# The place of operands and the order of six products in a trunk of split matmuls

## The chip, the cores and the metric

One core of a Trainium2 chip runs the whole program in one launch. The metric is the device time of one execution in microseconds; the median of three runs is compared.

## What is computed

One step of a decoder trunk of one layer, for 256 prompt tokens and 32 sample tokens (288 columns in all), width 2048:

```python
x = x + 0.5 * rmsnorm(swiglu(rmsnorm(x, g[0]), ffn1_w_in, ffn1_w_out), g[1])
m, sg, sh = hybrid_mixer(rmsnorm(x, g[2]), mix_w_in, ..., mix_w_out, s_gla, s_hgrn)
x = x + rmsnorm(m, g[3])
x = x + 0.5 * rmsnorm(swiglu(rmsnorm(x, g[4]), ffn2_w_in, ffn2_w_out), g[5])

def swiglu(x, w_in, w_out):
    gate, up = jnp.split(x @ w_in, 2, axis=-1)
    return (jax.nn.silu(gate) * up) @ w_out
```

All inputs are float32; the hidden width of the SwiGLU is 5632, and the mixer projects 2048 to 7184, runs two gated linear recurrences and projects back. Nearly all of the work is in these projections.

## The kernel before

**Tiling.** Activations stand transposed: a tile has 128 features on the partitions and the 288 tokens as columns. A weight unit is 1024 columns wide on 128 partitions: two k tiles of 512 output features each (or, in some stages, two times 256). It is loaded by SyncE into `raw`, and split into a high part, written by ScalarE as a rounded copy, and a low part, the rest, written by VectorE; both go into a `wh` buffer (four of them, and two more at stage borders). Activations are split in the same way, into `xh` and `xl` for the sixteen x tiles, and `hh` and `hl` for the four hidden tiles of a chunk of 512 hidden features.

**Products.** A block makes four output tiles (f = 0 to 3) of 128 features in four PSUM buffers. For each unit, each f and each k of the unit's two, `mm` records the three products of `mm3`: high weight by high x (L621), high weight by low x (L622), low weight by high x (L623). Each is one matmul of 288 columns with its own weight load. In some units (those named in `byk`, where tiles of x have only just been made, or evictions are still under way) k is the outer loop and f the inner one. The first units of two blocks at the borders between sub-layers are recorded by `Fill`, for x tiles that are early there. The FFN runs over eleven chunks: gate, up, and the output products of the chunk before.

**Places.** `columns` cuts the 288 columns into `PLACES` = 4 pieces of 72, and `turns_of` makes a matmul read four neighbouring columns (a `LINE` of four elements) of each piece in turn. `pairs` interleaves two k tiles, so that the pieces of one tile stand 144 elements apart. The results land in PSUM by the same pattern, 72 elements apart, and so in the natural order. The low tiles start one line behind the high ones, and unused elements (tiles named `gap`, and spare columns) set where the weights begin: in lines of four elements and modulo 16, a weight stands 6 lines behind the high x and 5 behind the low x that it meets.

**Order.** Each engine runs its list in the order in which the code recorded it; `tick` and `issue_after` interleave the other engines' work with a block's units.

Of the kernel before, what the change touches and what calls it, by code (L numbers as in the profile page):

```python
# [9 lines left out]
F32 = mybir.dt.float32  # L10
F32R = mybir.dt.float32r
# [5 lines left out]
P = 128  # L17
TP = 256
TS = 32
T = TP + TS  # L20
# [3 lines left out]
KT = D // P  # L24
# [6 lines left out]

RAW_BUFS = 3
HL_BUFS = 4
HALF = 1024 + 8
LINE = 4
PLACES = 4


def columns(t):

    return t.rearrange("p (g c) -> p g c", g=PLACES)


def turns_of(t):

    return t.rearrange("p g (i e) -> p i g e", e=LINE)


def pairs(pool, n, names):

    parts = []
    for at, name in zip((0, LINE), names):
        t = pool.tile([P, n * T + 16 * at], F32R, name=name, tag=name.split("_")[0])[:, at:at + n * T]
        t = t.rearrange("p (k g j c) -> p k g j c", g=PLACES, j=2, c=T // PLACES)
        parts.append([t[:, k // 2, :, k % 2, :] for k in range(n)])
    return parts

SCAN_LAG = 4
X_EARLY = 12


class Weights:


    def __init__(self, tc, rawp, hlp):
        self.tc, self.nc, self.rawp, self.hlp = tc, tc.nc, rawp, hlp
        self.srcs, self.raws, self.parts = [], {}, {}
        self.loaded = self.split = self.used = 0
        self.last = {}
        self.extra, self.extra_units = None, ()  # L70
        self.behind = None
# [2 lines left out]

        self.extra, self.extra_units = pool, units

    def add(self, src):
        self.srcs.append(src)

    def load(self):  # L80
        i, src = self.loaded, self.srcs[self.loaded]
# [27 lines left out]
    def pieces(self, n):  # L109

        i = self.split
        raw = self.raws.pop(i)
        pool = self.extra if i in self.extra_units else self.hlp
        hl = pool.tile([P, 2112], F32R, name=f"wh{i}", tag="wh")[:, 0:2 * HALF].rearrange("p (a c) -> p a c", a=2)
        h, l = hl[:, :, 0:512], hl[:, :, 512:1024]
        self.parts[i] = (h, l)
        self.split += 1
        raw = raw.rearrange("p (a b) -> p a b", b=512)
        for j in range(n):
            a = slice(0, 2) if n == 1 else slice(2 * j // n, 2 * j // n + 1)  # L120
            w = min(512, 1024 // n)
            c = slice(j * w % 512, j * w % 512 + w)
            i1 = self.nc.scalar.activation(h[:, a, c], raw[:, a, c], AF.Copy).ins  # L123
            i2 = self.nc.vector.tensor_tensor(l[:, a, c], raw[:, a, c], h[:, a, c].bitcast(F32), op=ALU.subtract).ins  # L124
            self.recent = i1, i2
            yield i1, i2
# [27 lines left out]
def trunk_kernel(ctx, tc, x_prompt, x_sample, state_gla, state_hgrn, norm_gains, f1_in, f1_out, f2_in, f2_out,  # L154
# [6 lines left out]
    xpool = ctx.enter_context(tc.tile_pool(name="xpool", bufs=1))  # L161
    rawp = ctx.enter_context(tc.tile_pool(name="rawp", bufs=RAW_BUFS))
    hlp = ctx.enter_context(tc.tile_pool(name="hlp", bufs=HL_BUFS))
    hlp.tile([P, 40], F32, name="gap_w", bufs=1)
    mmp = ctx.enter_context(tc.tile_pool(name="mmp", bufs=5, space=PSUM))
    aux = ctx.enter_context(tc.tile_pool(name="aux", bufs=3, space=PSUM))
    sqp = ctx.enter_context(tc.tile_pool(name="sqp", bufs=2))
# [34 lines left out]
    def block_units(w, col, k0, nk, width=512):  # L202
        per = 1024 // width
        for k in range(k0, k0 + nk, per):
            W.add(w[k * P:(k + per) * P, col:col + width].rearrange("(k p) c -> p k c", p=P))

    def pair_units(w, col0, col1, nk):

        for k in range(0, nk, 2):
            W.add([(256 * i, w[k * P:(k + 2) * P, c:c + 256].rearrange("(k p) c -> p k c", p=P))  # L210
                   for i, c in enumerate((col0, col1))])

    def ffn_ops():

# [56 lines left out]
    EARLY = 4  # L271
    x = [xpool.tile([P, T], F32, name=f"x{k}") for k in range(KT)]
    yg = [xpool.tile([P, 4, T], F32, name=f"y{k}") for k in range(4)]
    y = [yg[k // 4][:, k % 4, :] for k in range(KT)]
    xh, xl = pairs(xpool, KT, ("xh", "xl"))
    rt = xpool.tile([P, T], F32, name="rt")
    rp = xpool.tile([P, T], F32, name="rp")
    acc = xpool.tile([P, T], F32, name="acc")
# [256 lines left out]
    class Fill:  # L535
# [3 lines left out]
        def __init__(self, pool, name, gains, gnext, some, ahead):  # L539
            self.gnext, self.name, self.some, self.ahead = gnext, name, some, ahead  # L540
            pool.tile([P, 8], F32, name=f"{name}gap")

            self.tiles = [list(zip(*pairs(pool, EARLY, (f"{name}{n}h", f"{name}{n}l")))) for n in "xy"]
            self.gains = pool.tile([P, 24], F32, name=f"{name}g")[:, 0:EARLY]
            V.tensor_tensor(self.gains, gains[:, 0:EARLY], prm[:, gnext * KT:gnext * KT + EARLY], op=ALU.mult)

        def old(self):
# [63 lines left out]
    def block(name, nk, rhs, evac, width=512, tick=None, tail=1, hold=False, most=99, fill=None, late=0, byk=(), lag=0, skip=()):  # L611

        nf, per = width // P, 1024 // width
        nu = nk // per
        ps = [mmtile(f"{name}_{f}") for f in range(nf)]
        ws = [W.next() for _ in range(EARLY // per)] if fill else []

        def mm3(dst, w, f, k, parts, start, stop):
            a, c = k % per, slice(f * P, f * P + P)
            dst, parts = turns_of(columns(dst)), [turns_of(t) for t in parts]  # L620
            yield lambda: PE.matmul(dst, w[0][:, a, c], parts[0], start=start, stop=False)  # L621
            yield lambda: PE.matmul(dst, w[0][:, a, c], parts[1], start=False, stop=False)  # L622
            yield lambda: PE.matmul(dst, w[1][:, a, c], parts[0], start=False, stop=stop)  # L623

        def mm(w, f, k):
            if not fill or f or k >= EARLY:
                for ready in mm3(ps[f][:, 0:T], w, f, k, rhs(k), k == 0, k == nk - 1):
                    product[0] = ready().ins

        if fill:  # L630
            fill.products(lambda dst, k, parts, stop: mm3(dst, ws[k // per], 0, k, parts, k == 0, stop), ps[0][:, 0:T])
        for u in range(nu - tail):
            w = ws.pop(0) if ws else W.next()
            if u not in byk:
                for f in range(nf):
                    for k in range(u * per, (u + 1) * per):
                        mm(w, f, k)
                    if tick is not None and f % 2:
                        tick(u * per + f // 2)
            for k in range(u * per, (u + 1) * per) if u in byk else ():  # L640
                if fill and k < UPDATED:

                    fs = range(1 if k < EARLY else 0, nf)
                    threes = [list(mm3(ps[f][:, 0:T], w, f, k, rhs(k), k == 0, False)) for f in fs]
                    for three in threes:
                        three[0]()
                        product[0] = three[2]().ins
                    with tc.issue_after(product[0]):
                        for three in threes:
                            product[0] = three[1]().ins  # L650
                elif k < late:

                    threes = [list(mm3(ps[f][:, 0:T], w, f, k, rhs(k), k == 0, False)) for f in range(nf)]
                    for ready in [r for t in threes for r in t[:2]] + [t[2] for t in threes]:
                        product[0] = ready().ins
                else:
                    for f in range(nf):
                        mm(w, f, k)
                if tick is not None:
                    tick(k)  # L660
            if u not in skip and not (lag and u == nu - tail - 1):
                W.ahead(most)
            if fill and u == 5:
                fill.scaled()
        ws = [W.next() for _ in range(tail)]
        ks = range((nu - tail) * per, nk)
        ticked = 0
        for f in range(nf):
            for k in ks:
                mm(ws[k // per - (nu - tail)], f, k)  # L670
            ins = evac(f, fill.total(ps[f][:, 0:T]) if fill and f == 0 else ps[f][:, 0:T])
            while tick is not None and (ticked + 1) * nf <= (f + 1) * len(ks):
                tick(ks[ticked])
                ticked += 1
            if lag and f == lag:
                with tc.issue_after(ins):
                    W.ahead(most)
        if not hold:
            W.ahead()
# [4 lines left out]
    def ffn(tag, gcol, gnext, pn, before, fill=None):  # L684
# [2 lines left out]
        border = []  # L687
        with ExitStack() as pools:
            fp = pools.enter_context(tc.tile_pool(name=f"ffn{tag}", bufs=2))
            fp.tile([P, 24], F32, name=f"gap_f{tag}", bufs=1)  # L690
            hid, final_tiles = {}, []

            def do_in(c):
                hh, hl = pairs(fp, 4, (f"hh{tag}_{c}", f"hl{tag}_{c}"))
                hid[c] = (hh, hl)
                gs = []

# [1003 lines left out]
    class Border:  # L1701


        def __init__(self, n, gains, gnext, some, ahead=0):
            self.pools = ExitStack()
            top = self.pools.enter_context(tc.tile_pool(name=f"top{gnext}", bufs=1, side="right"))
            top.tile([P, 80], F32, name=f"gap{gnext}")
            W.begin_extra(self.pools.enter_context(tc.tile_pool(name=f"hx{gnext}", bufs=2, side="right")), wider(n))
            self.fill = Fill(self.pools.enter_context(tc.tile_pool(name=f"fl{gnext}", bufs=1, side="right")),
                             f"fill{gnext}", gains, gnext, some, ahead)  # L1710
# [47 lines left out]
```

## Time and profile before

| | |
|---|---|
| median of 3 runs | 2159.18 us (2158.32 to 2159.96) |
| the profiled execution | 2157.96 us |
| its span, first to last instruction | 2156.2 us |
| TensorE busy | 2144.9 us (99%) |
| VectorE busy | 1382.0 us (64%) |
| ScalarE busy | 1017.1 us (47%) |
| HBM over the span | 174 GB/s |
| mean granted TensorE clock | 1.000 |

Matmuls are pipelined: a row of the profile gives some 0.29 us for one, while the next begins about 0.13 us after it. The distance between starts is the figure to read. A name such as `wh<-raw` is the tile written and the tile read; L with a number is a line of the kernel, which for products is the line in `mm3`.

### The profile page before, as it was taken

Reading aid. Unit: us, or ns where it says so; the run is one execution under the profiler, and the core shown is the slowest. Engines: PE = TensorE matmul, PEld = TensorE weight load, DVE = VectorE, ACT = ScalarE, POOL = GpSimd, SP = SyncE. Lnnn points to the kernel's source line nnn. Section 1 sums busy time; section 2 is a strip of 40 time slices with the busy share of each in tenths; the row PEclk is TensorE's granted clock in tenths of the full one; section 3 lists DMA queues with packets and bytes.
Section 4 is the critical chain, followed back from the end, with each engine's and each line's share of the span. In section 5 each row is a group of like instructions: output and inputs, shape, how many; then the busy total and the mean of one; then the engine's idle time right before and its main releaser. Section 6 shows DMA issues by size and latency. Waiting matters only on the chain.

```text
span 2156.2 us, 43224 instructions
## 1 busy us (share of the span) xinstructions
PE 2144.9 (99%) x17828; PEld 2126.5 (99%) x17828; DVE 1382.0 (64%) x2253; ACT 1017.1 (47%) x1537; POOL 180.6 (8%) x327
## 2 busy tenths in 40 slices
PE   9999999999999999999999999999999999999998
PEld 9999999999999999999999999999999999999998
DVE  7656546555565568888888755854655466556656
ACT  6453433343344345655676654544434333433344
POOL 2000000000000001333210000000000020122005
PEclk9999999999999999999999999999999999999999
DMA  7655555555556554678666564556555665666556
GB/s 224 181 172 175 174 173 173 176 172 174 173 176 186 177 175 142 195 211 221 177 191 181 181 194 139 167 176 174 170 175 175 171 184 177 184 183 185 176 168 164
DMA packets 227334, 384.87 MB, mean 178 GB/s; under 512 B 21362, under 2 KB 60864, under 8 KB 227136
## 3 DMA queue, kind: packets, MB, share of 16 engines
q1 hardware_dynamic: 213872, 365.02, 57.0%
q0 software_dynamic: 10992, 16.77, 2.9%
q8 instruction: 140, 2.29, 0.4%
q10 hardware_dynamic: 2272, 0.31, 0.1%
q14 instruction: 58, 0.48, 0.1%
HBM read 363.75 MB, written 11.80 MB: 174 GB/s over the span
## 4 chain that ended last, share of the span: by engine, by line
PE 94%; DVE 3%; ACT 2%; DMA 1%; issue 1%; DVEq 0%; ACTq 0%; SPq 0%
PE gate L621 10%; PE gate L622 9%; PE gate L623 9%; PE out L621 8%; PE out L622 8%; PE out L623 8%; PE up L621 8%; PE up L622 8%; PE up L623 8%; PE hfq L621 2%; PE mo L621 1%; PE hfq L622 1%; PE hfq L623 1%; PE mo L623 1%; PE mo L622 1%; ACT wh L123 1%
## 5 line engine op out<-in xcount | busy, mean ns | idle before, releaser
L124 DVE TENSOR_TENSOR wh<-raw,wh 128x1024 fp32r<-128x1024 f32 (+1 forms) x676 | 822.1, 1217 | 579.9 <-ACT wh L123 577.7
L123 ACT ACTIVATE wh<-raw 128x1024 fp32r<-128x1024 f32 (+1 forms) x676 | 710.1, 1052 | 899.0 <-PE gate L623 282.5
L621 PE MATMUL gate<-xh,wh 128*128 128x288 f32 x1660 | 479.8, 290 | 0.6 <-ACT wh L123 0.4
L623 PE MATMUL gate<-xh,wh 128*128 128x288 f32 x1660 | 476.4, 288 | 0.0
L622 PE MATMUL gate<-xl,wh 128*128 128x288 f32 x1660 | 475.6, 289 | 0.1
L621 PE MATMUL up<-xh,wh 128*128 128x288 f32 x1408 | 406.8, 289 | 0.0
L621 PE MATMUL out<-hh,wh 128*128 128x288 f32 x1408 | 406.7, 289 | 0.0
L622 PE MATMUL up<-xl,wh 128*128 128x288 f32 x1408 | 405.9, 288 | 0.0
L622 PE MATMUL out<-hl,wh 128*128 128x288 f32 x1408 | 405.9, 288 | 0.0
L623 PE MATMUL up<-xh,wh 128*128 128x288 f32 x1408 | 405.8, 288 | 0.0
L623 PE MATMUL out<-hh,wh 128*128 128x288 f32 x1408 | 405.7, 288 | 0.0
L621 PEld LDWEIGHTS gate<-xh,wh 128*128 128x128 f32 x1660 | 311.0, 188 | 1.7 <-ACT wh L123 0.6
L622 PEld LDWEIGHTS gate<-xl,wh 128*128 128x128 f32 x1660 | 310.2, 188 | 1.1 <-DVE xl L287 0.8
L623 PEld LDWEIGHTS gate<-xh,wh 128*128 128x128 f32 x1660 | 311.0, 188 | 0.2 <-DVE wh L124 0.2
L623 PEld LDWEIGHTS up<-xh,wh 128*128 128x128 f32 x1408 | 264.3, 188 | 0.0
L623 PEld LDWEIGHTS out<-hh,wh 128*128 128x128 f32 x1408 | 264.3, 188 | 0.0
L621 PEld LDWEIGHTS out<-hh,wh 128*128 128x128 f32 x1408 | 264.2, 188 | 0.0
L621 PEld LDWEIGHTS up<-xh,wh 128*128 128x128 f32 x1408 | 264.2, 188 | 0.0
L622 PEld LDWEIGHTS up<-xl,wh 128*128 128x128 f32 x1408 | 264.1, 188 | 0.0
L622 PEld LDWEIGHTS out<-hl,wh 128*128 128x128 f32 x1408 | 264.0, 188 | 0.0
L807 DVE TENSOR_TENSOR y<-out,y 128x288 f32<-128x288 f32 x287 | 118.4, 452 | 75.7 <-PE out L623 75.6
L764 POOL DMA_DIRECT2D xT<-b x64 | 37.2, 588 | 739.1 <-PE gate L623 553.7
(417 smaller groups left out, 2542.5 us busy)
## 6 DMA issues: line engine op xcount, KB each, us to landing
raw<-in_ffn_w_in_dram SPq DMA_DIRECT2D x350, 512.0 KB, 3.7
raw<-in_ffn_w_out_dram SPq DMA_DIRECT2D x176, 512.0 KB, 3.6
raw<-in_mix_w_in_dram SPq DMA_DIRECT2D x64, 512.0 KB, 4.4
raw<-in_mix_w_in_dram SPq DMA_DIRECT2D x96, 256.0 KB, 3.3
raw<-in_mix_w_out_dram SPq DMA_DIRECT2D x32, 512.0 KB, 3.7
out_dram<-s POOLq DMA_DIRECT2D x32, 256.0 KB, 3.0
s<-in_state_gla_dram SPq DMA_DIRECT2D x16, 256.0 KB, 5.8
s<-in_state_hgrn_dram SPq DMA_DIRECT2D x16, 256.0 KB, 5.8
```

Of the source, the lines that this page charges most:

```text
L123: i1 = self.nc.scalar.activation(h[:, a, c], raw[:, a, c], AF.Copy).ins
L124: i2 = self.nc.vector.tensor_tensor(l[:, a, c], raw[:, a, c], h[:, a, c].bitcast(F32), op=ALU.subtract).ins
L621: yield lambda: PE.matmul(dst, w[0][:, a, c], parts[0], start=start, stop=False)
L622: yield lambda: PE.matmul(dst, w[0][:, a, c], parts[1], start=False, stop=False)
L623: yield lambda: PE.matmul(dst, w[1][:, a, c], parts[0], start=False, stop=stop)
L764: queues[n % len(queues)].dma_start(dst[q * TS:(q + 1) * TS, 4 * g:4 * g + 4, :, cols].rearrange("p k t c -> p (k t) c"), b32[rows, q])
L807: V.tensor_tensor(y[k], ps, y[k], op=ALU.add)
```

## The change

`PLACES` becomes 8: a piece has 36 columns, and four k tiles share a block of eight pieces (`tiles` takes the place of `pairs`), the pieces of one tile again 144 elements apart. High and low parts, and odd and even k tiles, become four regions of one buffer: `xhl` for x, and `hid` for the hidden values, where both chunks in flight are now in one buffer instead of two. The regions begin 4 or 6 lines apart (modulo 16): the odd high tiles at 0, the even high tiles at 4, both low regions at 10. `PART` is the place of a tile inside its block of four.

A weight buffer gets four regions too (odd high, odd low, even high, even low), and `Weights.add` is told the unit's k, so that each unit begins 7, 2, 0 or 9 lines on (`AHEAD_LINES`), following the place of its two x tiles.

`two` records the six products of two k tiles of one f as one row: odd k with high and low x, then even and odd in turn. It is used where f is the outer loop, and in a block's last units. `mm3` still serves the by-k units and the fills, with the tiles in their new places.

```diff
-HALF = 1024 + 8
 LINE = 4
-PLACES = 4
+PLACES = 8
+ODD_HIGH, ODD_LOW, EVEN_LOW = 1536 + 6 * LINE, 512 + LINE, 1024 + 5 * LINE
+PART = (0, 3, 1, 2)
+AHEAD_LINES = (7, 2, 0, 9)
...
-def pairs(pool, n, names):
-
-    parts = []
-    for at, name in zip((0, LINE), names):
-        t = pool.tile([P, n * T + 16 * at], F32R, name=name, tag=name.split("_")[0])[:, at:at + n * T]
-        t = t.rearrange("p (k g j c) -> p k g j c", g=PLACES, j=2, c=T // PLACES)
-        parts.append([t[:, k // 2, :, k % 2, :] for k in range(n)])
-    return parts
+def tiles(pool, n, name):
+
+    q = n // 2 * T
+    t = pool.tile([P, LINE + 10 * LINE + 4 * q], F32R, name=name, tag=name, bufs=1)
+    hs, ls = [None] * n, [None] * n
+    for dst, odd, at in ((hs, 1, 0), (hs, 0, q + 4 * LINE), (ls, 1, 2 * q + 10 * LINE), (ls, 0, 3 * q + 10 * LINE)):
+        r = t[:, LINE + at:LINE + at + q].rearrange("p (b g j c) -> p b g j c", g=PLACES, j=4, c=T // PLACES)
+        for u in range(n // 2):
+            dst[2 * u + odd] = r[:, u // 4, :, PART[u % 4], :]
+    return hs, ls
...
+def apart(t, step):
+
+    return bass.AP(t.tensor, t.offset, [list(t.ap[0]), [step, 2], list(t.ap[1])])
...
-    def add(self, src):
+    def add(self, src, k):
         self.srcs.append(src)
+        self.at.append(LINE * AHEAD_LINES[k // 2 % 4])
...
-        hl = pool.tile([P, 2112], F32R, name=f"wh{i}", tag="wh")[:, 0:2 * HALF].rearrange("p (a c) -> p a c", a=2)
-        h, l = hl[:, :, 0:512], hl[:, :, 512:1024]
+        hl = pool.tile([P, 2112], F32R, name=f"wh{i}", tag="wh")
+        at = self.at[i]
+        low = hl[:, at + ODD_LOW:at + ODD_LOW + 2 * (EVEN_LOW - ODD_LOW)]
+        l = low.rearrange("p (a c) -> p a c", a=2)[:, ::-1, 0:512]
+        h = apart(hl[:, at:at + 512], ODD_HIGH)
...
-    xh, xl = pairs(xpool, KT, ("xh", "xl"))
+    xh, xl = tiles(xpool, KT, "xhl")
...
-            self.tiles = [list(zip(*pairs(pool, EARLY, (f"{name}{n}h", f"{name}{n}l")))) for n in "xy"]
+            both = list(zip(*tiles(pool, 2 * EARLY, f"{name}hl")))
+            self.tiles = [both[:EARLY], both[EARLY:]]
...
+        def two(w, f, k):
+            if fill and not f and k < EARLY:
+                return
+            dst, c = turns_of(columns(ps[f][:, 0:T])), slice(f * P, f * P + P)
+            (eh, el), (oh, ol) = ([turns_of(t) for t in rhs(k + j)] for j in range(2))
+            six = [(0, 1, oh), (0, 1, ol), (0, 0, eh), (1, 1, oh), (0, 0, el), (1, 0, eh)]
+            for n, (low, a, part) in enumerate(six):
+                product[0] = PE.matmul(dst, w[low][:, a, c], part, start=k == n == 0, stop=k == nk - 2 and n == 5).ins
...
                 for f in range(nf):
-                    for k in range(u * per, (u + 1) * per):
-                        mm(w, f, k)
+                    two(w, f, u * per)
...
-            for k in ks:
-                mm(ws[k // per - (nu - tail)], f, k)
+            for k in ks[::per]:
+                two(ws[k // per - (nu - tail)], f, k)
...
+            hidden = tiles(fp, 8, f"hid{tag}")
...
-                hh, hl = pairs(fp, 4, (f"hh{tag}_{c}", f"hl{tag}_{c}"))
+                hh, hl = (t[c % 2 * 4:c % 2 * 4 + 4] for t in hidden)
```

The rest of the diff sizes the gap tiles so that all units keep the same places modulo 16 lines.

TensorE before, in a gate block of the second chunk, from the end of one unit (`wh_1776`) into the next (`wh_1805`); `gate_2_0` is the output tile, and the three figures behind 128 are the read pattern, sweeps by places by line:

```order
L623 MATMUL gate_2_3_1693<-xh,wh_1776 128x18x4x4
L621 MATMUL gate_2_0_1690<-xh,wh_1805 128x18x4x4 [waits Activation_49]
L622 MATMUL gate_2_0_1690<-xl,wh_1805 128x18x4x4
L623 MATMUL gate_2_0_1690<-xh,wh_1805 128x18x4x4 [waits DVE_49]
L621 MATMUL gate_2_0_1690<-xh,wh_1805 128x18x4x4
```

TensorE now, in a unit of the same block (all six are of one line, and alike ones are counted):

```order
L647 MATMUL gate_2_0_1681<-xhl,wh_1610 128x9x8x4 x3
L647 MATMUL gate_2_0_1681<-xhl,wh_1610 128x9x8x4 [waits DVE_49]
L647 MATMUL gate_2_0_1681<-xhl,wh_1610 128x9x8x4 x2
L647 MATMUL gate_2_1_1682<-xhl,wh_1610 128x9x8x4 x6
L647 MATMUL gate_2_2_1683<-xhl,wh_1610 128x9x8x4 x6
```

The wait for VectorE's low part has moved from the third product of a unit to the fourth, and the pattern reads 9 sweeps of 8 places instead of 18 of 4.

ScalarE before, where a chunk's first hidden tile is written between the splits of units (`wh` from `raw`):

```order
L123 ACTIVATE wh_6702<-raw_6618 128x2x512
L123 ACTIVATE wh_6731<-raw_6647 128x2x512
L123 ACTIVATE wh_6760<-raw_6676 128x2x512
L718 ACTIVATE hh_8_6308<-u 128x4x72
L123 ACTIVATE wh_6809<-raw_6705 128x2x512
```

ScalarE now, at the same place:

```order
L137 ACTIVATE wh_6681<-raw_6597 128x2x512
L137 ACTIVATE wh_6710<-raw_6626 128x2x512
L137 ACTIVATE wh_6739<-raw_6655 128x2x512
L742 ACTIVATE hid_206<-u 128x8x36
L137 ACTIVATE wh_6788<-raw_6684 128x2x512
```

No instruction has moved here; the hidden tile is written in eight pieces of 36 instead of four of 72.

More of the change, by code (lines that the diff above doesn't have):

```diff
@@ L66, in __init__ @@
         self.tc, self.nc, self.rawp, self.hlp = tc, tc.nc, rawp, hlp
-        self.srcs, self.raws, self.parts = [], {}, {}
+        self.srcs, self.at, self.raws, self.parts = [], [], {}, {}
         self.loaded = self.split = self.used = 0
@@ L163, in trunk_kernel @@
     hlp = ctx.enter_context(tc.tile_pool(name="hlp", bufs=HL_BUFS))
-    hlp.tile([P, 40], F32, name="gap_w", bufs=1)
+    hlp.tile([P, 48], F32, name="gap_w", bufs=1)
     mmp = ctx.enter_context(tc.tile_pool(name="mmp", bufs=5, space=PSUM))
@@ L204, in block_units @@
         for k in range(k0, k0 + nk, per):
-            W.add(w[k * P:(k + per) * P, col:col + width].rearrange("(k p) c -> p k c", p=P))
+            W.add(w[k * P:(k + per) * P, col:col + width].rearrange("(k p) c -> p k c", p=P), k)
     def pair_units(w, col0, col1, nk):
@@ L210, in pair_units @@
             W.add([(256 * i, w[k * P:(k + 2) * P, c:c + 256].rearrange("(k p) c -> p k c", p=P))
-                   for i, c in enumerate((col0, col1))])
+                   for i, c in enumerate((col0, col1))], k)
     def ffn_ops():
@@ L541, in __init__ @@
             pool.tile([P, 8], F32, name=f"{name}gap")
-            self.tiles = [list(zip(*pairs(pool, EARLY, (f"{name}{n}h", f"{name}{n}l")))) for n in "xy"]
-            self.gains = pool.tile([P, 24], F32, name=f"{name}g")[:, 0:EARLY]
+            both = list(zip(*tiles(pool, 2 * EARLY, f"{name}hl")))
+            self.tiles = [both[:EARLY], both[EARLY:]]
+            self.gains = pool.tile([P, 32], F32, name=f"{name}g")[:, 0:EARLY]
             V.tensor_tensor(self.gains, gains[:, 0:EARLY], prm[:, gnext * KT:gnext * KT + EARLY], op=ALU.mult)
@@ L689, in ffn @@
             fp = pools.enter_context(tc.tile_pool(name=f"ffn{tag}", bufs=2))
-            fp.tile([P, 24], F32, name=f"gap_f{tag}", bufs=1)
+            fp.tile([P, 32], F32, name=f"gap_f{tag}", bufs=1)
             hid, final_tiles = {}, []
+            hidden = tiles(fp, 8, f"hid{tag}")
             def do_in(c):
-                hh, hl = pairs(fp, 4, (f"hh{tag}_{c}", f"hl{tag}_{c}"))
+                hh, hl = (t[c % 2 * 4:c % 2 * 4 + 4] for t in hidden)
                 hid[c] = (hh, hl)
@@ L1706, in __init__ @@
             top = self.pools.enter_context(tc.tile_pool(name=f"top{gnext}", bufs=1, side="right"))
-            top.tile([P, 80], F32, name=f"gap{gnext}")
+            top.tile([P, 88], F32, name=f"gap{gnext}")
             W.begin_extra(self.pools.enter_context(tc.tile_pool(name=f"hx{gnext}", bufs=2, side="right")), wider(n))
```

## Prediction

> **What bounds the kernel now.** I read the page first (busy shares, granted clock, chain), then the waits of the matmul engine, then its timeline product by product, because the whole case lies in the step from one product to the next.
>
> ```profile
> PE 2144.9 (99%) x17828; PEld 2126.5 (99%) x17828; DVE 1382.0 (64%) x2253; ACT 1017.1 (47%) x1537; POOL 180.6 (8%) x327
> PEclk9999999999999999999999999999999999999999
> PE 94%; DVE 3%; ACT 2%; DMA 1%; issue 1%; DVEq 0%; ACTq 0%; SPq 0%
> PE warm L335 <- POOL onesD L257: 1.1, 1, 1.1
> PE sc L1123 <- DVE k_g L1186: 0.9, 2, 0.7
> PE postf L863 <- DVE sq L803: 0.5, 2, 0.3
> ```
>
> TensorE is busy from end to end at the full granted clock, it makes 94% of the chain, and its longest waits are 1.1, 0.9 and 0.5 us. So no wait is worth anything here; only the number of products or the time of one product moves the end. The number is fixed by three lines of the helper that records the products. Restricted to one of these lines, the view of stretches gives the count in brackets behind TensorE's busy time (L621, L622 and L623 in this order):
>
> ```profile
> 0.00:2156.20 2156.20, 1557.58 (x5384) 1009.13 (x5384) 1.00 0.61 178
> 0.00:2156.20 2156.20, 1546.77 (x5384) 1007.56 (x5384) 1.00 0.61 178
> 0.00:2156.20 2156.20, 1549.46 (x5384) 1010.03 (x5384) 1.00 0.61 178
> ```
>
> That is 3 x 5384 = 16152 products of 288 columns. The 0.29 us that a row shows for one is no price, since products overlap; the price is the distance of starts. From the timeline, the first and the last of 25 rows each (24 distances, one weight unit's worth): an output stage, a gate stage with x operands, and a gate stage that takes the unit tile by tile ("by k").
>
> ```profile
> 1890.02 0.29 PE L621 MATMUL out<-hh,wh 128*128 128x288 f32 x1
> ...
> 1893.06 0.29 PE L621 MATMUL out<-hh,wh 128*128 128x288 f32 x1
> 1206.73 0.29 PE L621 MATMUL gate<-xh,wh 128*128 128x288 f32 x1
> ...
> 1209.77 0.29 PE L621 MATMUL gate<-xh,wh 128*128 128x288 f32 x1
> 1211.67 0.29 PE L621 MATMUL gate<-xh,wh 128*128 128x288 f32 x1
> ...
> 1214.73 0.29 PE L621 MATMUL gate<-xh,wh 128*128 128x288 f32 x1
> ```
>
> The first two take 3.04 us, 126.67 ns for one product, to the last digit alike although their operands lie in different tiles. The third takes 3.06 us, 127.5 ns, with the same layout and another order. All products at 126.67 ns make 16152 x 126.67 = 2046 us of the span of 2156.2; the other 110 us are the small matmuls of the scans, start and end, which the change leaves alone.
>
> **The layout's price so far.** The trace has a few products of the same 288 columns whose moving operand lies in one run, with no places:
>
> ```profile
> 53.25 0.29 PE L489 MATMUL pre<-nh,onesR 128*128 128x288 f32 x1
> 53.38 0.29 PE L489 MATMUL pre<-nl,onesR 128*128 128x288 f32 x1
> 53.51 0.27 PE L430 MATMUL tp_prm<-ident,stage 128*128 128x128 f32 x1
> 926.61 0.30 PE L1443 MATMUL hms<-nh,ones 128*128 128x288 f32 x1
> 926.74 0.29 PE L1443 MATMUL hms<-nl,ones 128*128 128x288 f32 x1
> 926.87 0.29 PE L621 MATMUL v<-xh,wh 128*128 128x288 f32 x1
> ```
>
> Two of them take 0.26 us both times, 130 ns each, 3.33 ns more than the products that read four places in turn. They stand alone between other kinds, so some of the 3.33 may be the change of kind. It is the nearest row there is to "what places are worth".
>
> **The change part by part.**
>
> 1. *Eight places instead of four.* Both patterns read four neighbouring columns, then jump 144 elements. Before, a sweep has 4 jumps and there are 18 sweeps; now 8 and 9. The results land with the same pattern, 36 columns apart instead of 72. Instructions and columns are the same. From one run to four places, two doublings, the rows show -3.33 ns, 1.67 for a doubling. Bounds for the third doubling: the whole step once more (-3.33 ns) at the good end, the whole step given back (+3.33 ns, 130 ns again) at the bad one; nothing in the trace excludes a loss.
>
> 2. *The order of six, and the places of weights beside x.* Two tiles' six products now go odd-high, odd-low, even-high, odd-high, even-low, even-high by their x, with the start of each x 6, 6 and 4 lines lower (modulo 16) than the one before, a line being the kernel's LINE, four elements; till now the starts moved by one or two lines up and down. The by-k row shows that order alone is worth something: 127.5 against 126.67 ns, 0.83 ns, though all its tiles stand as in the other rows. So this part can go either way by about that much. I take nothing for it by itself, and keep -0.83 and +0.83 inside the bounds of part 1.
>
> 3. *How many products get it.* Counted in the changed program's list of TensorE, the new loop issues 15456 of 16152 products. The other 696 (by-k units, early fills) keep the order of three, on the new places. At +-3.33 ns these are 2.3 us at most; I take nothing.
>
> 4. *Waits.* In front of a unit's first products stand ScalarE's high half and VectorE's low half. The low half is now needed at the fourth product instead of the third, 127 ns later; the first product needs the high halves of both tiles, which one ScalarE instruction writes. Nothing queued behind them changes: ScalarE, VectorE, SyncE and GpSimd issue the same instructions, apart from two neighbours that change places, and no DMA moves. The cover is large:
>
> ```profile
> L124 DVE TENSOR_TENSOR wh<-raw,wh 128x1024 fp32r<-128x1024 f32 (+1 forms) x676 | 822.1, 1217 | 579.9 <-ACT wh L123 577.7
> L123 ACT ACTIVATE wh<-raw 128x1024 fp32r<-128x1024 f32 (+1 forms) x676 | 710.1, 1052 | 899.0 <-PE gate L623 282.5
> ACT wh L123 <- PE gate L623: 282.5, 147, 2.0
> ACT wh L123 <- PE up L623: 232.5, 120, 2.0
> ACT wh L123 <- PE out L623: 222.9, 118, 2.1
> ```
>
> A unit's split takes 1.05 us on ScalarE, then 1.22 on VectorE, of 3.04 us that TensorE spends on it, and ScalarE stands waiting for TensorE to free a buffer (up to 2.1 us at a time). The split's pieces are as large as before and only lie elsewhere (the high ones 1560 elements apart, the low ones in falling order); even if it became a third slower (+0.4 us on VectorE) it would stay hidden. Price zero; cover gone, it would show as TensorE waiting for wh.
>
> 5. *One tile for high and low, both chunks of hidden values.* If the dependency tracking took the whole tile for one thing, an output stage would wait for the next chunk's last hidden value. The built program has no such wait: the releasers of TensorE's waits are the same kinds in nearly the same numbers. Price zero.
>
> **The sum.** 15456 x 1.67 ns = 25.8 us. The profiled execution took 2157.96 us (2156.2 span, 1.8 around it): 2157.96 - 25.8 = 2132.2. The median of the three runs lies 1.2 us above it (0.06%): 2133.
>
> The Trainium skill (TensorE: Matmul & The Clock Gate, Back-to-back issue gap) gives N / 2.4 + 2.5 ns for a warm stream, 122.5 ns at 288 columns, as I work it out. The trace has 126.67 at full clock, so by that page 4.17 ns a product could still go, 64 us over the 15456, and the time would be near 2095. No row here shows a 288-column product that fast, so this is no end of my range.
>
> **The rivals.**
>
> *More than one doubling's worth.* The hand-over from product to product is mostly a matter of where the next operand starts, and order and places together take 3.33 ns or more. For it: the row of by-k units, where order alone moved the price. Against it: three sorts of hand-over (x up a line, down a line, to the next tile) live side by side in the steady units and still sum to a flat 3.04. Time: 2159.2 - 15456 x 3.33 ns = 2108.
>
> *Nothing happens.* 126.67 ns is a fixed cost of each product and its own weight load, and layout does not touch it. For it: the same 3.04 us with operands from the x tiles and from the hidden tiles, to the last digit. Against it: 130 ns and 127.5 ns in rows with the same number of columns. Time: 2159, and within 4.3 us of it. The Trainium skill (SBUF — State Buffer, Who interferes with whom) says that moving operand and weights come through two independent ports; by that rule, where a weight stands beside its x does nothing. This trace cannot tell, since all its units stand alike.
>
> *Slower: the longer jump between operands costs at every hand-over.* x starts now jump by 4 to 6 lines instead of 1 or 2, and each sweep spreads over twice the range in both memories. It is decided at the six products of two tiles: above 760 ns (6 x 126.67) it is this rival. For it: the one other order in the trace is slower, not faster, +0.83 ns; 15456 x 0.83 = 12.8 us gives 2172. At its far end, 130 ns, 2159.2 + 51.5 = 2211. Against it: more jumps went with less time so far. The Trainium skill (Advanced Engine Details and Errata, PSUM Cachelines) says that non-contiguous patterns slow matmuls while every two consecutive elements should adjoin. Both kernels write runs of four, so the trace's four-place rows, faster than the one-run rows, speak against reading it as a charge on jumps.
>
> *A stall of supply* (part 4 or 5 wrong) would show as TensorE waiting; with idle time of 2 us a unit I give it 2 in 100, inside the slower case.
>
> **How the numbers follow.** Chances: gain of about one doubling (0.3 to 2.5 ns a product) 0.38; more than that 0.22; nothing 0.14; slower 0.26. A measurement of this kernel tells about 0.2%, 4.3 us, which is 0.28 ns a product. So faster 0.60, same 0.14, slower 0.26. The likeliest case alone reaches from 2120 to 2153. The range for 8 in 10 takes in nearly all of the big gain (down to 2092, 4.3 ns a product) and the slower case to a little beyond its nearer price: 2178 (+1.2 ns a product), leaving out some 5 in 100 below and 10 above.
>
> **What would show it.** In a steady stretch of an output stage, 24 products in 3.00 us (125.0 ns): forecast. 2.96 or less: the bigger gain. 3.04: nothing. 3.06 or more: slower. The distances should be the same in output and gate stages, since both have the same places modulo 16 lines; if they differ, something other than the relation of x and weight decides. The by-k units should stay within 3.0 to 3.1 us. No row of TensorE's waits should be above 2 us, and the split of a unit near 1.05 and 1.22 us. The prediction fails if a product's distance does not follow the number of places, that is, if the 3.33 ns between one run and four places was only the price of a change of kind.

## The result, and the profile after

The changed kernel takes 2147.65 us (median of four runs, 2146.85 to 2148.18) against 2159.18: a ratio of 0.9946 (95% interval 0.9929 to 0.9964), 11.5 us less. The forecast was 2133, 26 us less. The direction was right, the size more than twice too large.

The page of the changed kernel, same rows as before:

```profile
PE 2134.7 (99%) x17828; PEld 2115.5 (99%) x17828; DVE 1379.6 (64%) x2253; ACT 1016.8 (47%) x1537; POOL 180.5 (8%) x327
PEclk9999999999999999999999999999999999999999
PE 93%; DVE 3%; ACT 2%; issue 1%; DMA 1%; POOL 0%; DVEq 0%; ACTq 0%; POOLq 0%
L138 DVE TENSOR_TENSOR wh<-raw,wh 128x1024 fp32r<-128x1024 f32 (+1 forms) x676 | 821.4, 1216 | 572.2 <-ACT wh L137 571.2
L137 ACT ACTIVATE wh<-raw 128x1024 fp32r<-128x1024 f32 (+1 forms) x676 | 709.9, 1052 | 886.5 <-PE gate L647 275.9
```

The other engines do what they did: the split of a unit still takes 1.05 and 1.22 us, and the granted clock is 0.999. The span shrank by 10.1 us and TensorE's busy time by 10.2. TensorE's longest waits and the count of products from the new loop:

```profile
PE o L1394 <- ACT kd L1502: 1.2, 1, 1.2
PE warm L349 <- POOL onesD L271: 1.1, 1, 1.1
PE sc L1147 <- DVE k_g L1210: 1.0, 2, 0.8
0.00:2156.20 2156.20, 1969.95 (x15456) 1953.54 (x15456) 1.00 0.60 178
```

So all of the gain is in the distance of products. The timeline now merges products of one line, so that a whole gate block of 192 products (eight units) is one row. Here are the gate and up blocks of the sixth chunk, after the change; the starts of the same two blocks before; and then, in the changed kernel again, the starts of five units that follow each other (the first column; the rest of such a row covers only the one or two products in view there):

```profile
351.04 24.38 PE L647 MATMUL gate<-xhl,wh 128*128 128x288 f32 x192
375.25 24.38 PE L647 MATMUL up<-xhl,wh 128*128 128x288 f32 x192
```

```profile
352.26 0.29 PE L621 MATMUL gate<-xh,wh 128*128 128x288 f32 x1
376.58 0.29 PE L621 MATMUL up<-xh,wh 128*128 128x288 f32 x1
```

```profile
351.04 0.42 PE L647 MATMUL gate<-xhl,wh 128*128 128x288 f32 x2
354.04 0.41 PE L647 MATMUL gate<-xhl,wh 128*128 128x288 f32 x2
357.02 0.41 PE L647 MATMUL gate<-xhl,wh 128*128 128x288 f32 x2
360.11 0.41 PE L647 MATMUL gate<-xhl,wh 128*128 128x288 f32 x2
363.15 0.42 PE L647 MATMUL gate<-xhl,wh 128*128 128x288 f32 x2
```

A block went from 24.32 us to 24.21 (126.67 to 126.1 ns a product). Inside it, units of 24 products take 3.00, 2.98, 3.09 and 3.04 us (2.996, 2.988, 3.082 and 3.040 from the starts in nanoseconds), and this repeats through the kernel. The second kind is 124.5 ns a product, below what the prediction took as the new price; the third is above the old price of 3.04. A hidden stage shows the same in a milder form, two kinds of unit in turn:

```profile
471.89 0.41 PE L647 MATMUL out<-hid,wh 128*128 128x288 f32 x2
474.88 0.43 PE L647 MATMUL out<-hid,wh 128*128 128x288 f32 x2
477.90 0.41 PE L647 MATMUL out<-hid,wh 128*128 128x288 f32 x2
480.89 0.43 PE L647 MATMUL out<-hid,wh 128*128 128x288 f32 x2
```

These take 2.99, 3.02, 2.99 us. The first one here (part 1 of the block, after part 2) is of the same part as the slow third unit above (part 1, after part 3). So the part alone does not make a unit slow. In the steady state six products of one f take 747 ns everywhere except in those third and fourth units, whatever the first six of a unit takes: read from the starts in nanoseconds, the third unit's last three sixes take 785, 755 and 786 ns, the fourth's first two 771 and 773.

### The profile page after: what moved, and what is told of

It is laid out like the page before. It is cut to its first block, busy times and chain, and to the rows that moved or that the text cites. A ratio compares the mean times of both kernels' runs of the same rounds, so it can differ in the third digit from the quotient of the medians.

```text
span 2146.1 us, 43224 instructions
## 1 busy us (share of the span) xinstructions
PE 2134.7 (99%) x17828; PEld 2115.5 (99%) x17828; DVE 1379.6 (64%) x2253; ACT 1016.8 (47%) x1537; POOL 180.5 (8%) x327
## 4 chain that ended last, share of the span: by engine, by line
PE 93%; DVE 3%; ACT 2%; issue 1%; DMA 1%; POOL 0%; DVEq 0%; ACTq 0%; POOLq 0%
PE gate L647 26%; PE out L647 24%; PE up L647 24%; PE hfq L647 5%; PE mo L647 4%; PE hi L647 2%; PE v L647 2%; ACT wh L137 1%; DVE wh L138 1%; PE gate L637 1%; PE gate L636 0%; PE gate L638 0%; PE os L1401 0%; PE sc L1147 0%; ACT ls L202 0%
## 5 line engine op out<-in xcount | busy, mean ns | idle before, releaser
L647 PE MATMUL gate<-xhl,wh 128*128 128x288 f32 x4584 | 588.3, 288 | 1.2 <-DVE u L740 0.8
L647 PEld LDWEIGHTS gate<-xhl,wh 128*128 128x128 f32 x4584 | 582.0, 187 | 2.8 <-issue 0.7
L647 PE MATMUL out<-hid,wh 128*128 128x288 f32 x4224 | 532.5, 286 | 0.0
L647 PEld LDWEIGHTS out<-hid,wh 128*128 128x128 f32 x4224 | 530.2, 187 | 0.1
L647 PE MATMUL up<-xhl,wh 128*128 128x288 f32 x4152 | 527.9, 287 | 0.0
L647 PEld LDWEIGHTS up<-xhl,wh 128*128 128x128 f32 x4152 | 525.3, 187 | 0.0
L647 PE MATMUL hfq<-xhl,wh 128*128 128x288 f32 x768 | 103.3, 290 | 0.0
L647 PEld LDWEIGHTS hfq<-xhl,wh 128*128 128x128 f32 x768 | 98.6, 187 | 0.9
L647 PE MATMUL mo<-xhl,wh 128*128 128x288 f32 x768 | 97.6, 288 | 0.2 <-ACT y L1715 0.2
L647 PEld LDWEIGHTS mo<-xhl,wh 128*128 128x128 f32 x768 | 97.1, 187 | 0.5 <-ACT y L1715 0.4
```

What stands on the lines that cost most here:

```text
L647: product[0] = PE.matmul(dst, w[low][:, a, c], part, start=k == n == 0, stop=k == nk - 2 and n == 5).ins
```

## The experiments

The theory after this reading is called A; its rivals are called B and C, and each expectation says anew what they are and what times they give. A: places, order and weights together bring the six from 760 to 747 ns, and what is lost again is lost at the border between units, where x jumps from the last tile of one unit to the first of the next (the jump is told in lines modulo 16).

**Order of the units' places.** The parts are taken in falling order, and the weights follow.

```diff
-PART = (0, 3, 1, 2)
-AHEAD_LINES = (7, 2, 0, 9)
+PART = (0, 3, 2, 1)
+AHEAD_LINES = (7, 2, 9, 0)
```

> The changed kernel with its tiles' places in a block of four taken in falling order, PART (0, 3, 2, 1) instead of (0, 3, 1, 2), and the weights following, (7, 2, 9, 0). In the changed kernel a gate or up unit of 24 products takes 2.996, 2.988, 3.082 or 3.040 us by its place in the row of four, where six products in the steady state take 747 ns (2.988 for 24). Theory A, the jump from the last x of one unit to the first x of the next decides: the jumps, modulo 16 lines, become 7, 3, 3, 3 instead of 7, 10, 5, 10, and jump 3 costs 3 ns in the output stages (750 ns for the first six). Then all four kinds of x unit take 2.988 to 2.992 us, some 147 ns less for four, 17 us over 470 units: 2130 us. Theory B, the place itself decides (parts 1 and 2 are slow beside their weights): nothing changes but which unit is slow, 2146 to 2149 us. Theory C, time is lost to an engine or a wait that falls on the third unit of four: the third stays at 3.08 us, 2147 us.

Measured: 2138.63 us, ratio to the kernel before 0.9901 (0.9886 to 0.9916). Its gate and up blocks, and the starts of five units:

```profile
349.24 24.15 PE L647 MATMUL gate<-xhl,wh 128*128 128x288 f32 x192
373.23 24.15 PE L647 MATMUL up<-xhl,wh 128*128 128x288 f32 x192
```

```profile
349.24 0.43 PE L647 MATMUL gate<-xhl,wh 128*128 128x288 f32 x2
352.25 0.41 PE L647 MATMUL gate<-xhl,wh 128*128 128x288 f32 x2
355.23 0.43 PE L647 MATMUL gate<-xhl,wh 128*128 128x288 f32 x2
358.24 0.41 PE L647 MATMUL gate<-xhl,wh 128*128 128x288 f32 x2
361.23 0.43 PE L647 MATMUL gate<-xhl,wh 128*128 128x288 f32 x2
```

No unit is slow any more: 3.01, 2.98, 3.01, 2.99. The unit of part 1, 3.08 before, is now the fourth, comes after part 2 and takes 2.99. So neither B nor C is the cause of the slow third unit. A's price was too low, though: the same jump of 3 lines costs 20 ns more when it enters parts 2 and 0 than when it enters part 1. It is a loss of the first six alone (769 ns, then 747), so the modulo-16 jump is not the whole rule; 9 us came instead of 17. Three of the four jumps changed at once here, so the 9 us belong to the three together.

**Order of three on the new places.**

```diff
-                    two(w, f, u * per)
+                    for k in range(u * per, (u + 1) * per):
+                        mm(w, f, k)
...
-            for k in ks[::per]:
-                two(ws[k // per - (nu - tail)], f, k)
+            for k in ks:
+                mm(ws[k // per - (nu - tail)], f, k)
```

> The changed kernel with the old order of products (high by high, high by low, low by high, tile after tile) on the new places. Theory A, places and order work only together: the order of three makes jumps of +6 and +4 lines as well as falls; the by-k units of the changed kernel, which have that order, take 3.08 us for 24, 128.3 ns a product. At that price 15456 products take 33 us more than in the changed kernel: 2175 to 2185 us, slower than the kernel before. Theory B, the prediction's: eight places are worth what they are by themselves, order costs up to 0.83 ns: at most 13 us more than the changed kernel, 2147 to 2161 us.

Measured: 2189.61 us, ratio 1.0135 (1.0120 to 1.0150). The block's two starts:

```profile
357.40 0.29 PE L636 MATMUL gate<-xhl,wh 128*128 128x288 f32 x1
...
382.10 0.29 PE L636 MATMUL up<-xhl,wh 128*128 128x288 f32 x1
```

24.70 us, 128.6 ns a product, 2 ns worse than four places with that order. On the new places, with their new offsets, the old order is a loss: theory A. Eight places on the old offsets were not run, so the loss can't be put down to their number alone.

**The row of six on the old places.** The kernel before, with `two` of the change and its two calls.

```diff
+        def two(w, f, k):
...
-                    for k in range(u * per, (u + 1) * per):
-                        mm(w, f, k)
+                    two(w, f, u * per)
```

> The kernel before with the new row of six products on its old places (four pieces, old weights). Theory A (jumps decide): the x starts move by +1, -3, +2, -1, -1, +2 lines, all small as before, so the distance stays near 126.67 ns: 2155 to 2165 us. Theory B (the order alone brings the gain, for instance since two products in a row use one weight tile): near the changed kernel, 2148 us or less. Theory C (any other order on the old places is bad, as in the by-k units): 127.5 ns, 2172 us.

Measured: 2175.05 us, ratio 1.0070 (1.0055 to 1.0085).

```profile
355.20 0.29 PE L632 MATMUL gate<-xh,wh 128*128 128x288 f32 x1
...
379.74 0.29 PE L632 MATMUL up<-xh,wh 128*128 128x288 f32 x1
```

24.54 us, 127.8 ns: theory C. Small jumps between x starts do not make an order good; here A's measure was wrong. On the old places the new order alone costs 1.1 ns.

**Four places with the new regions and order.**

```diff
-PLACES = 8
+PLACES = 4
-PART = (0, 3, 1, 2)
-AHEAD_LINES = (7, 2, 0, 9)
+PART = (0, 1)
+AHEAD_LINES = (7, 9, 7, 9)
...
-        r = ...rearrange("p (b g j c) -> p b g j c", g=PLACES, j=4, c=T // PLACES)
+        r = ...rearrange("p (b g j c) -> p b g j c", g=PLACES, j=2, c=T // PLACES)
...
-            dst[2 * u + odd] = r[:, u // 4, :, PART[u % 4], :]
+            dst[2 * u + odd] = r[:, u // 2, :, PART[u % 2], :]
```

> The changed kernel with four places instead of eight: the same four regions with the same offsets modulo 16 lines, the same row of six, pieces of 72 columns and blocks of two tiles, weights following by 0 or 2 lines. The prediction's theory (a doubling of the places is the gain): the steady six go back to 760 ns, 2159 us or more. Rival (the falling starts are the gain, the number of places is not): the steady six stay at 747 ns, and the time is at or below the changed kernel's, 2130 to 2148 us, by what its unit jumps (14 and 10 lines modulo 16) cost. Third case: the offsets suit eight places alone and four places lose with them: above 2165 us.

Measured: 2221.41 us, ratio 1.0282 (1.0265 to 1.0300), the third case.

```profile
362.55 25.20 PE L647 MATMUL gate<-xhl,wh 128*128 128x288 f32 x192
387.58 24.68 PE L647 MATMUL up<-xhl,wh 128*128 128x288 f32 x188
```

The block takes 25.03 us from start to start (the last four products of the second row lie outside the view), 130.4 ns. With the new order and offsets eight places are needed. With the old order it is the other way round: four places on the old offsets take 126.67 ns, eight on the new ones 128.6. `PLACES` sets the pattern in PSUM as well as that of x, and no run parts the two.

**Rising order of parts.** `PART = (0, 1, 2, 3)`, `AHEAD_LINES = (7, 0, 9, 2)` in the changed kernel.

> The changed kernel with the tiles' places rising, PART (0, 1, 2, 3), weights following, (7, 0, 9, 2). Jumps between units, modulo 16 lines: 5, 5, 5, 1 where the changed kernel has 7, 10, 5, 10. By the units of the changed kernel jump 5 costs 29 ns (3.017 us for 24, hidden tiles) and jump 1 costs 24 ns, and only jump 10 into part 1 (a third unit after a second) locks a unit at 3.08. Theory A (the jump into the unit decides): no unit above 3.02 us, x units 3.016 on average against 3.026, 2143 us. Theory B (the places of parts 1 and 2 are bad in themselves): some units stay at 3.04 to 3.08, 2147 us or more.

Measured: 2146.41 us, ratio 0.9940 (0.9926 to 0.9955). Its two blocks:

```profile
351.23 24.26 PE L647 MATMUL gate<-xhl,wh 128*128 128x288 f32 x192
375.33 24.26 PE L647 MATMUL up<-xhl,wh 128*128 128x288 f32 x192
```

That is 24.10 us a block, and the four kinds of x unit take 2.99, 3.01, 3.04 and 3.01. No unit stays at 3.08, and where a unit starts badly its last two sixes are back at 747; the unit that enters part 2 loses more than A had for its jump. The time lies between what A and B gave, and by time alone this run does not tell them apart.

**Weights that do not follow.** The kernel with falling units, every unit's weights 7 lines on.

```diff
-AHEAD_LINES = (7, 2, 9, 0)
+AHEAD_LINES = (7, 7, 7, 7)
```

> The kernel with falling units (2138.6 us) with its weights no longer following x: every unit begins 7 lines on, (7, 7, 7, 7). Only units at part 0 keep their relation of weight and x; the others have the weights 5 lines further, 2 lines back and 7 lines further against x. Theory A (only the starts of x matter, weights come by a port of their own): 2138 to 2140 us. Theory B (the place of a weight beside the x that is read while it loads matters): the three other parts lose their steady 747 ns for six; at the by-k price of 128.3 ns a product three quarters of 15456 products lose 3.8 ns, 44 us: 2165 to 2190 us.

Measured: 2169.01 us, ratio 1.0045 (1.0030 to 1.0059), 30 us above the kernel with falling units.

**All x four lines on.** The kernel with falling units, x, hidden and fill tiles moved by four lines, a gap ahead of the weights shortened by as much.

```diff
-    t = pool.tile([P, LINE + 10 * LINE + 4 * q], F32R, name=name, tag=name, bufs=1)
+    t = pool.tile([P, 5 * LINE + 10 * LINE + 4 * q], F32R, name=name, tag=name, bufs=1)
...
-        r = t[:, LINE + at:LINE + at + q]...
+        r = t[:, 5 * LINE + at:5 * LINE + at + q]...
...
-    hlp.tile([P, 48], F32, name="gap_w", bufs=1)
+    hlp.tile([P, 32], F32, name="gap_w", bufs=1)
```

> The kernel with falling units with all x, hidden and fill tiles four lines further on, weights where they were: every relation of weight and x moves by four lines modulo 16 (0, 6, 11 become 12, 2, 7), no jump between x starts changes, nor does any between weights. Theory A (weights do not matter): 2138 to 2140 us. Theory B (they do): all steady sixes change alike; slower by up to 44 to 59 us at the by-k price, 2180 to 2200 us; faster only if 0, 6, 11 was not the best.

Measured: 2194.75 us, ratio 1.0164 (1.0149 to 1.0180), 56 us above the kernel with falling units, and every kind of unit is slow (3.08 to 3.11 us). The blocks of both runs, the weights that do not follow first:

```profile
354.69 24.57 PE L647 MATMUL gate<-xhl,wh 128*128 128x288 f32 x192
379.11 24.57 PE L647 MATMUL up<-xhl,wh 128*128 128x288 f32 x192
```

```profile
359.56 24.98 PE L647 MATMUL gate<-xhl,wh 128*128 128x288 f32 x192
384.37 24.98 PE L647 MATMUL up<-xhl,wh 128*128 128x288 f32 x192
```

24.42 us (127.2 ns) and 24.81 us (129.2 ns) against 23.99. In the second nothing but the place of x against weights differs: same pattern, same jumps, same engines' lists. The first run moved the weights and left x, the second moved x and left the weights, and both lose, so the relation of the two is the likely cause; a run that moves both alike was not made. What B builds on here is thus real, though it did not make the third unit slow: where a weight stands beside x is worth up to 4.3 ns a product.

The run with weights that do not follow holds a test of its own. Only the units of part 0 keep their relation there. The starts of five units, of parts 0, 3, 2, 1 and 0:

```profile
354.69 0.41 PE L647 MATMUL gate<-xhl,wh 128*128 128x288 f32 x2
357.68 0.42 PE L647 MATMUL gate<-xhl,wh 128*128 128x288 f32 x2
360.76 0.41 PE L647 MATMUL gate<-xhl,wh 128*128 128x288 f32 x2
363.83 0.43 PE L647 MATMUL gate<-xhl,wh 128*128 128x288 f32 x2
366.90 0.41 PE L647 MATMUL gate<-xhl,wh 128*128 128x288 f32 x2
```

Part 0 still takes 2.99 us, the other parts 3.08, 3.07 and 3.07. And when x steps from part 1 to part 0 inside the block, the first six takes 749 ns here, against 769 or 770 for the same step of x in the kernel with falling units. So the cost at a border hangs on the weights too, and A, which counts the jump of x alone, does not explain it.

**Twice the same part.** The kernel with falling units, x units placed so that two neighbours have the same part, in two blocks.

```diff
+X_PLACE = (0, 4, 1, 5, 2, 6, 3, 7)
...
-            dst[2 * u + odd] = r[:, u // 4, :, PART[u % 4], :]
+            dst[2 * u + odd] = r[:, place[u] // 4, :, PART[place[u] % 4], :]
...
-        self.at.append(LINE * AHEAD_LINES[k // 2 % 4])
+        self.at.append(LINE * AHEAD_LINES[place[k // 2 % 8] % 4])
```

> The kernel with falling units, in which x units take the same part of both blocks in turn (parts 0, 0, 3, 3, 2, 2, 1, 1); hidden tiles as they were. Four of eight unit borders then have the jump of 12 lines that also stands inside a unit, the others 7, 3, 3, 3. There the x units take 2.986, 3.009, 2.990 and 3.008 us, 20 ns more for a step from an even place to an odd one. Theory A (the jump alone sets the price at a border): the repeats cost nothing, 2.987 us, so eight units save some 40 ns, 2 to 3 us over 470 units: 2136 us. Theory B (the price hangs on the part itself): 2138 to 2139 us.

Measured: 2135.99 us, ratio 0.9892 (0.9877 to 0.9907). This is the fastest version, 11.7 us under the changed kernel. Its interval overlaps that of the kernel with falling units, but the block shows where the rest came from:

```profile
348.69 24.10 PE L648 MATMUL gate<-xhl,wh 128*128 128x288 f32 x192
372.63 24.10 PE L648 MATMUL up<-xhl,wh 128*128 128x288 f32 x192
```

23.94 us against 23.99. Units that repeat a part take 2.986 or 2.987 us, nothing lost at the border, as A expected.

## Why the prediction was right or wrong

*What bounds the kernel* held: no wait gained or lost anything, and the distance of products carries the whole result.

*Part 1, the price of a doubling*, is the step that failed. Its 1.67 ns came from comparing a one-run product between other kinds with four places in a stream, and it made the number of places a quantity with a price of its own. The rows did not carry it: in nanoseconds the two pairs take 261 and 267, not 260 each, and one-run products of that trace with no wait behind them run from 127 to 139 ns. Nor does the number of places have one price that adds to the rest. With the old order, eight places on the new offsets cost 128.6 ns and four on the old ones 126.67. With the new order and offsets, four cost 130.4 ns and eight 126.1 over the same block. The sentence that named what would make the forecast fail, "if a product's distance does not follow the number of places", is what these runs showed.

*Part 2, nothing for the order and the weights' places*, failed with it. The order alone on the old places costs +1.1 ns (15.2 us: 2175.05 against 2159.83 for the kernel before in the same series), and four lines more between weights and x cost 4.3 ns. Neither could be summed with the other.

*The size.* The steady six went from 760 to 747 ns, 2.17 ns a product, more than the 1.67 taken. At 15456 products that is 33.5 us; 11.5 came. Most of the other 22 us stays at the borders between units, a term that the sum did not have: counted over the starts of all products, the units that no other matmul interrupts lose 17 us against the steady 747 ns. The largest share, some 12 us, is the third unit of four in gate and up blocks, 94 ns over 2.988 us, and the fourth, 52 ns over; output stages lose 3. The rest lies in interrupted units, by-k units and the small matmuls. Falling places, without the jump that enters the third unit, brought 9.0 us, repeating parts the next 2.6, of which 1.0 may lie between the two series of runs (2159.83 and 2158.82 us for the kernel before). The 122.5 ns of the prediction's aside was reached by no unit here; the fastest took 124.4.

*Part 3*: the by-k units did not stay as they were; in whole units that nothing interrupts the distance is 128.3 to 128.8 ns, where it was 127.3 to 128.1, and all 696 products lose some 1.5 us. Too small to matter.

*Parts 4 and 5* (waits, the split, one tile for both chunks) were right, as the rows after show.

*The rivals.* "Nothing happens" rested on 3.04 us being the same for operands in different tiles. But all units had been given the same places modulo 16 lines, so the agreement could not show that places do not matter, and the shifted runs show that they do. The Trainium skill's independent ports (SBUF — State Buffer, Who interferes with whom) would have the shift of x against weights cost nothing; here it costs 56 us, and the measurement decides. "More than one doubling's worth" came nearer, since it took order and places together; but its 3.33 ns was too much even for the steady units (2.17), it missed the borders, and it put all on where the next operand starts, while the shift of x against weights, with the same jumps, costs 4.3 ns. "Slower" did not come, but it is what the halves do: the new order on the old places, the old order on the new places, and four places with the rest new are all slower than the kernel before. The test in the last paragraph, that output and gate stages should agree, fell (125.2 against 126.1 ns), and it pointed to the borders at once. The output stage alone met the forecast of 125.0 ns, but by luck: units of 2.99 and 3.02 us in turn, a larger gain and a loss that the sum did not know.

## What to carry to other kernels

Where TensorE is busy to the last per cent, measure the distance of starts over a whole number of units, by unit and by stage, and look at every transition that a layout makes, not only at the steady one. Places, order and weight offsets are one choice: a part of it tried alone can lose although the whole gains, so change them together or do not judge by the parts. A steady price multiplied by the count of products is only a ceiling; the borders between units gave back about half of it here (17 of 33.5 us).

## What the runs showed of the hardware that was not expected

A stream of matmuls with 288 columns of float32r has no single price at full clock: the same count of columns ran at 124.5 ns in the best units, and at 126.67, 127.8, 128.6, 129.2 and 130.4 ns a product over whole blocks, by read pattern, addresses and order. A bad start can last: after the jump from part 3 to part 1 the whole unit of 24 stays slow (785 and 755 ns for six, in turn by f), and the next unit recovers only after two sixes; the same unit entered from part 2 shows 750 and then 747. Why the weights' places beside x are good and four lines further on bad, and why entering parts 0 and 2 costs 20 ns once in the kernel with falling units and entering parts 1 and 3 next to nothing, stays open; no run here tells whether reads of x or of the weights lose the time.
